# Seven-product blocks for six of the eight column blocks of an MLP's first matrix, in three passes between pieces of the second

## The chip, the cores and the metric

The kernel runs on one core of one Trainium2 chip. The metric is device time in microseconds of one execution. Three runs of the kernel before gave 2460.88 (median), 2460.5 and 2461.72 us.

## The reference

A decoder trunk of two layers on 256 tokens of width 2048, in float32: differential attention, then an MLP; a Mamba-2 mixer, then an MLP. Every sub-layer has an RMS norm ahead of it and a residual behind it. What the change touches is the MLP, which is there twice:

```python
D_MODEL = 2048; SEQ = 256; D_FF = 4 * D_MODEL
def sq_relu_mlp(h, w1, w2):
    return jnp.square(jax.nn.relu(h @ w1)) @ w2
...
h = h + sq_relu_mlp(rms_norm(h, mlp_norm[i]), mlp_w1[i], mlp_w2[i])
```

So per MLP: (256 x 2048) @ (2048 x 8192), a squared ReLU, then (256 x 8192) @ (8192 x 2048).

## The kernel before

**Precision.** Every weight tile is split in two float32r parts: `split_weights` lets ScalarE cast 128 x 1024 elements to the high part (L155) and VectorE subtract it from the raw tile for the low part (L156). Activations are split likewise (`split_pair`, L244 and L245). A product is then three: high x high, activation low x weight high, activation high x weight low.

**The wide form of the first matrix.** `wide_one` and `sub_part` compute one block of 128 hidden columns for all 256 tokens: weights stationary, activations streaming, 16 k-steps. Each k-step is one matmul over 512 columns (high and low activations side by side, L166) and one over 256 (L170). The outcome has hidden units on partitions, as the second matrix needs it. `add_sums` adds the two halves.

**The seven-product form.** For 1024 hidden columns, tokens, inner dimension and columns are each cut in half, and seven products take the place of eight, as in Strassen's scheme in Winograd's variant. `sum_parts` forms the four sums of activations (S1 to S4, split, eight tiles `sa`). `seven` takes 256 rows of the matrix at a time: it loads four 512-column pieces, forms four sums of weights on VectorE (L547 to L550), splits all seven (L540, L541) and issues 7 x 3 matmuls of 512 columns into seven open sums in seven of the eight PSUM banks (L554 to L556). `seven_out` combines them on VectorE (L567 to L573). The outcome has tokens on partitions, so `hidden` applies the squared ReLU (L587) and transposes it on PE, 16 transposes per 1024 columns (L597).

**The order of an MLP.** Four quarters `q` of 2048 hidden columns each. In the first half of a quarter, the eight calls of `seven` for one column block of 1024 alternate with the eight wide blocks of another. Half of the first matrix is so computed by seven products. In the second half, `token_block` multiplies the hidden tiles by the second matrix: for each of four column groups j, eight pieces of 128 x 1024 weights, 12 matmuls of 512 columns each (L227, L229), and VectorE adds the outcome to the residual h (L636).

**Queues.** `side.tick()` runs a step of waiting side work (the sums of activations, `hidden`, the norms) at fixed points of the program. Tiles are named by a tag and a number of buffers: `raw` (loaded weights) and `w` (split weights) have four each, `raw7` two; PSUM has four banks `mm`, three `aux` and one `aux1`. The build lays out each engine's instructions in a fixed order: the program's order is the priority, and an instruction whose inputs or buffer would not be ready yet lets later ones go ahead. All weight loads are issued in order on SP's queue.

Of the kernel before, what the change touches and what calls it, by code (L numbers as in the profile page):

```python
# [12 lines left out]
F32 = mybir.dt.float32  # L13
# [7 lines left out]
P = 128  # L21
# [11 lines left out]
HPG = 8  # L33
SP = 64
MASKED = -1.0e30


C_MIX0, C_MLP0, C_MIX1, C_MLP1 = 0, 16, 32, 48
# [10 lines left out]
def bc(ap, n):  # L49

    return ap.unsqueeze(1).broadcast_to([ap.shape[0], n, ap.shape[1]])
# [31 lines left out]
def wait(n):  # L83
    for _ in range(n):
        yield
# [3 lines left out]
def trunk_kernel(ctx: ExitStack, tc: tile.TileContext, x, xt, par, rope, qk, wv, wo, w10, w10s, w20, win, wdt, wout, w11, w11s, w21, out):  # L89
# [99 lines left out]
    def wide_pair(src, b, acts):  # L189
# [7 lines left out]
                    sub_part(w[t], acts, 8 * s, pp[t], i, s == 0, s == 1)  # L197
        return pp

    def wide_one(src, b, acts):  # L200
        pp = bank()
        raw = [load(src[b, s]) for s in range(2)]
        for s in range(2):
            sub_block(split_weights(raw[s]), acts, 8 * s, pp, s == 0, s == 1)
        return pp
# [4 lines left out]
            S.copy(out=dst[:, t, :], in_=pp[t][:, 1, :])  # L210
            V.tensor_tensor(out=dst[:, t, :], in0=pp[t][:, 0, :], in1=dst[:, t, :], op=ALU.add)

    def token_block(src, j, acts):

        pp = [bank().rearrange("p a b -> p (a b)") for _ in range(2)]
        n = len(src)
        for s in range(n):
            w = split_weights(load(src[s][j]))
            for i, wi in enumerate(w):
                for k in range(2):  # L220
                    while len(acts) <= 2 * s + k:
                        side.tick()
                    act = acts[2 * s + k]
                    m = wi[:, k * NB:(k + 1) * NB]
                    for t in range(2):
                        tok = slice(t * P, (t + 1) * P)
                        PE.matmul(pp[t], lhsT=act[:, 0, tok], rhs=m, start=(s + i + k == 0), stop=(s == n - 1 and i + k == 2))  # L227
                        if i == 0:
                            PE.matmul(pp[t], lhsT=act[:, 1, tok], rhs=m, start=False, stop=False)  # L229
                    if i == 0 or k:  # L230
                        side.tick()
        return pp

    def rng(src, a, b):
# [270 lines left out]

    def sum_parts(pool, x, dst):

        a = pool.tile([P, 2, T], F32, tag="relu", bufs=2, name="a")
        for i in range(2):
            V.tensor_tensor(out=a[:, i, :], in0=x[i][:, 0, :].bitcast(F32), in1=x[i][:, 1, :].bitcast(F32), op=ALU.add)  # L510
        a11, a21, a12, a22 = (a[:, i, t * P:(t + 1) * P] for i in range(2) for t in range(2))
        f = pool.tile([P, 4, P], F32, tag="relu", bufs=2, name="asum")
        yield
        V.tensor_tensor(out=f[:, 0, :], in0=a21, in1=a22, op=ALU.add)
        V.tensor_tensor(out=f[:, 1, :], in0=f[:, 0, :], in1=a11, op=ALU.subtract)
        V.tensor_tensor(out=f[:, 2, :], in0=a11, in1=a21, op=ALU.subtract)
        V.tensor_tensor(out=f[:, 3, :], in0=a12, in1=f[:, 1, :], op=ALU.subtract)
        yield
        sa = pool.tile([P, 2, 4, P], F32R, tag="sa", bufs=8, name="sa")
        S.copy(out=sa[:, 0], in_=f)  # L520
        V.tensor_tensor(out=sa[:, 1], in0=f, in1=sa[:, 0].bitcast(F32), op=ALU.subtract)
        x0, x1 = x
        s1, s2, s3, s4 = ([sa[:, i, n, :] for i in range(2)] for n in range(4))
        dst.append([[x0[:, i, 0:P] for i in range(2)], s4, [x1[:, i, 0:P] for i in range(2)], s1, s3, s2, [x1[:, i, P:T] for i in range(2)]])
        yield

    def seven(pool, src, acts, pp, start, stop):


        r = pool.tile([P, 7, NB], F32, tag="raw7", bufs=2, name="raw7")  # L530
        nc.sync.dma_start(out=r[:, 0:3, :], in_=src[:, 0:3, :])
        nc.sync.dma_start(out=r[:, 6, :], in_=src[:, 3, :])
        ws = []

        def parts(a, n):
            if n == 2:
                w = wp.tile([P, 2, 2, NB], F32R, tag="w", bufs=4, name="w")
            else:
                w = pool.tile([P, 2, 1, NB], F32R, tag="w1", bufs=2, name="w1")
            S.copy(out=w[:, 0], in_=r[:, a:a + n, :])  # L540
            V.tensor_tensor(out=w[:, 1], in0=r[:, a:a + n, :], in1=w[:, 0].bitcast(F32), op=ALU.subtract)  # L541
            for i in range(n):
                ws.append((w[:, 0, i, :], w[:, 1, i, :]))

        parts(0, 2)

        V.tensor_tensor(out=r[:, 3:5, :], in0=r[:, 0:2, :], in1=bc(r[:, 6, :], 2), op=ALU.subtract)  # L547
        parts(2, 2)
        V.tensor_tensor(out=r[:, 5, :], in0=r[:, 1, :], in1=r[:, 3, :], op=ALU.add)
        V.tensor_tensor(out=r[:, 6, :], in0=r[:, 5, :], in1=r[:, 2, :], op=ALU.subtract)  # L550
        parts(4, 2)
        parts(6, 1)
        for n, ((ah, al), (wh, wl)) in enumerate(zip(acts, ws)):
            PE.matmul(pp[n], lhsT=ah, rhs=wh, start=start, stop=False)  # L554
            PE.matmul(pp[n], lhsT=al, rhs=wh, start=False, stop=False)  # L555
            PE.matmul(pp[n], lhsT=ah, rhs=wl, start=False, stop=stop)  # L556
            if n in (1, 3, 5, 6):
                side.tick()

    def seven_out(pool, pp):  # L560

        p1, p3, p2, p5, p7, p6, p4 = pp
        u = pool.tile([P, 2, 2, NB], F32, tag="raw7", bufs=2, name="u")
        a = pool.tile([P, NB], F32, tag="relu", bufs=2, name="ua")
        b = pool.tile([P, NB], F32, tag="relu", bufs=2, name="ub")
        S.copy(out=a, in_=p1)
        V.tensor_tensor(out=u[:, 0, 0], in0=p2, in1=a, op=ALU.add)  # L567
        V.tensor_tensor(out=a, in0=p6, in1=a, op=ALU.add)
        V.tensor_tensor(out=b, in0=p7, in1=a, op=ALU.add)
        V.tensor_tensor(out=u[:, 0, 1], in0=a, in1=p5, op=ALU.subtract)  # L570
        V.tensor_tensor(out=u[:, 0, 1], in0=p3, in1=u[:, 0, 1], op=ALU.add)
        V.tensor_tensor(out=u[:, 1, 1], in0=b, in1=p5, op=ALU.subtract)
        V.tensor_tensor(out=u[:, 1, 0], in0=b, in1=p4, op=ALU.subtract)  # L573
        return u

    def mlp(xs, w1, w1s, w2, pool, after):
        r2 = const.tile([P, 2], F32, tag="r2", bufs=2, name="r2")
# [5 lines left out]
                    yield  # L583
                yield from sum_parts(pool, xs[2 * j:2 * j + 2], sas)

        def hidden(u, hid):
            V.scalar_tensor_tensor(out=u, in0=u, scalar=0.0, in1=u, op0=ALU.max, op1=ALU.mult)  # L587
            yield from wait(2)
            uf = u.rearrange("p t a b -> p t (a b)")
            for j in range(0, 4, 2):  # L590
                axs = []
# [7 lines left out]
                for ax in axs:  # L599
                    hid += split_pair(ax)  # L600
                    yield

        side.add(sums_of(), slow=True)
        for q in range(4):
            hid = []
            p7 = None
            wait_for = 2 if q == 0 else 0
            for j in range(8 + wait_for):
                if j >= wait_for:
                    i = j - wait_for  # L610
                    while len(sas) <= i:
                        side.tick()
                    if i == 0:
                        p7 = [t for _ in range(3) for t in (bank().rearrange("p a b -> p (a b)"), aux())] + [aux1()]
                    seven(pool, w1s[q, i], sas[i], p7, i == 0, i == 7)
                    if i == 7:
                        u = seven_out(pool, p7)
                if j < 8:
                    if j % 2 == 0:
                        r = pool.tile([P, 2, T], F32, tag="relu2", bufs=1, name="relu")  # L620
                    if q or j > 1:
                        add_sums(r[:, j % 2:j % 2 + 1], [wide_one(w1, 8 * q + j, xs)])
                    elif j == 0:
                        add_sums(r, wide_pair(w1, 0, xs))
                    if j % 2:
                        if q == 0 and j == 1:
                            norm_mean()
                            V.reciprocal(out=r2, in_=ms)
                        V.scalar_tensor_tensor(out=r, in0=r, scalar=0.0, in1=r, op0=ALU.max, op1=ALU.mult)
                        hid += split_pair(r)  # L630
            side.add(hidden(u, hid))
            for j in range(4):
                src = rng(w2, 8 * q + 4, 8 * q + 8) + rng(w2, 8 * q, 8 * q + 4)
                pp = token_block(src, j, hid)
                for t in range(2):
                    V.scalar_tensor_tensor(out=h[:, t, cols(j)], in0=pp[t], scalar=r2[:, t:t + 1], in1=h[:, t, cols(j)],  # L636
                                           op0=ALU.mult, op1=ALU.add)
                    if q == 3:
                        after(j, t)

    xs_next = []

# [267 lines left out]
    return _units(b)  # L910


def _mixed(w):

    b = w.reshape(2048, 4, 2, 1024)
    blocks = _blocks(np.ascontiguousarray(b[:, :, 1]).reshape(2048, 4096))
    c = b[:, :, 0].reshape(8, 2, P, 4, 2, 512).transpose(3, 0, 2, 1, 4, 5)
    s = np.stack([c[:, :, :, 0, 0], c[:, :, :, 1, 1], c[:, :, :, 1, 0], c[:, :, :, 0, 1]], axis=3)
    return blocks, np.ascontiguousarray(s)


def _tokens(w):
# [71 lines left out]
```

## Time and profile before

| what | value |
|---|---|
| median of three runs | 2460.88 us |
| the profiled execution's own time | 2460.63 us |
| its span | 2458.7 us |
| busy: PE, VectorE (DVE), ScalarE (ACT) | 100%, 80%, 57% |
| moved by DMA | 471.21 MB, mean 192 GB/s |
| granted TensorE clock | 1.000 |
| first MLP, roughly | 405 to 1100 us |
| second MLP, roughly | 1767 us to the end |

Durations come from the profiled execution. PE's matmuls overlap, so that a matmul's own duration (about 390 ns for 512 columns) is longer than the distance to the next one; the chain of waits gives the distances. PEld are weight loads, which run beside the matmuls. The chain lists, in order of time, the work that ended last; a wait lists who waited for whom.

### The profile page before, as it was taken

To read this page: it belongs to the slowest core of one execution; us is meant where nothing else is said; L and a number is where in the kernel's file an instruction comes from. 1 tells how busy PE (TensorE), PEld (TensorE's weight loads), DVE (VectorE), ACT (ScalarE), POOL (GpSimd) and SP (SyncE) were. 2 spreads that over 40 slices of the span, in tenths; PEclk is the share of its full clock that TensorE was granted. 3 is DMA by queue.
4 is the path that set the end of the run, shared out by engine and by line. 5 is a ranking of instruction groups with operands and counts; after the bars stand their busy time and mean duration, and the time that the engine had idled before them with its cause. 6 is when DMAs were issued, how large, how long until landed. Compare 5 with 4: busy or idle time off the path is not lost.

```text
span 2458.7 us, 33143 instructions
## 1 busy us (share of the span) xinstructions
PE 2452.2 (100%) x12486; PEld 2079.7 (85%) x12486; DVE 1962.1 (80%) x2565; ACT 1406.3 (57%) x2014; POOL 1.2 (0%) x8
## 2 busy tenths in 40 slices
PE   9999999999999999999999999999999999999999
PEld 8888888888888888888888888888888888888887
DVE  6988879977958859758886887887997796795874
ACT  7666656545535536556776575775664454553553
POOL 0000000000000000000000000000000000000000
PEclk9999999999999999999999999999999999999999
DMA  7445555565565655556565555556566556565554
GB/s 271 162 163 180 172 185 181 183 234 194 196 199 189 206 178 199 176 176 208 196 197 192 176 197 197 167 191 210 171 204 217 190 184 214 189 206 197 182 185 156
DMA packets 132128, 471.21 MB, mean 192 GB/s; under 512 B 14752, under 2 KB 14944, under 8 KB 131968
## 3 DMA queue, kind: packets, MB, share of 16 engines
q1 hardware_dynamic: 129248, 460.38, 56.1%
q10 hardware_dynamic: 2720, 8.71, 1.1%
q8 instruction: 98, 1.61, 0.3%
q14 instruction: 62, 0.51, 0.1%
HBM read 466.88 MB, written 2.16 MB: 191 GB/s over the span
## 4 chain that ended last, share of the span: by engine, by line
PE 100%; ACT 0%; DVE 0%; DVEq 0%; issue 0%
PE pp L227 28%; PE pp L166 26%; PE pp L229 14%; PE pp L170 13%; PE aux L554 2%; PE aux L555 2%; PE aux L556 2%; PE pp L555 2%; PE pp L554 2%; PE pp L556 2%; PE aux L796 1%; PE pp L337 1%; PE aux L597 1%; PE aux L428 0%; PE aux L138 0%; PE aux L273 0%
## 5 line engine op out<-in xcount | busy, mean ns | idle before, releaser
L156 DVE TENSOR_TENSOR w<-raw,w 128x1024 fp32r<-128x1024 f32 x730 | 885.4, 1222 | 334.6 <-ACT w L155 332.1
L155 ACT CAST w<-raw 128x1024 fp32r<-128x1024 f32 x730 | 762.4, 1052 | 542.5 <-PE pp L227 433.3
L227 PE MATMUL pp<-w,act 128*128 128x512 f32 x3072 | 957.1, 391 | 0.6 <-ACT w L155 0.6
L166 PE MATMUL pp<-act,w 128*128 128x512 f32 x2768 | 679.3, 392 | 0.0
L227 PEld LDWEIGHTS pp<-w,act 128*128 128x128 f32 x3072 | 575.2, 188 | 120.3 <-issue 1.0
L229 PE MATMUL pp<-w,act 128*128 128x512 f32 x1536 | 598.4, 390 | 0.0
L166 PEld LDWEIGHTS pp<-act,w 128*128 128x128 f32 x2768 | 507.2, 188 | 99.8 <-issue 1.0
L170 PEld LDWEIGHTS pp<-act,w 128*128 128x128 f32 x2768 | 362.6, 191 | 17.9 <-issue 0.9
L170 PE MATMUL pp<-act,w 128*128 128x256 f32 x2768 | 373.2, 283 | 0.0
L540 ACT CAST w<-raw 128x1024 fp32r<-128x1024 f32 (+1 forms) x256 | 241.1, 945 | 200.4 <-PE pp L170 105.7
L229 PEld LDWEIGHTS pp<-w,act 128*128 128x128 f32 x1536 | 288.5, 188 | 58.2
L541 DVE TENSOR_TENSOR w<-raw,w 128x1024 fp32r<-128x1024 f32 (+1 forms) x256 | 272.3, 1087 | 41.5 <-ACT w L540 38.5
L547 DVE TENSOR_TENSOR raw<-raw 128x1024 f32<-128x1024 f32 x64 | 78.1, 1221 | 3.5 <-DMA raw<-in_w11s 1.5
L554 PE MATMUL aux<-w,sa 128*128 128x512 f32 x192 | 75.0, 391 | 0.0
L555 PE MATMUL aux<-w,sa 128*128 128x512 f32 x192 | 74.9, 390 | 0.0
L556 PE MATMUL aux<-w,sa 128*128 128x512 f32 x192 | 74.7, 389 | 0.0
L721 DVE SCALAR_TENSOR_TENSOR cy<-u,cwb,cy 128x256 f32<-128x256 f32 x144 | 63.6, 482 | 9.9 <-ACT cy L719 9.6
L210 ACT COPY relu<-pp 128x256 f32<-128x256 f32 x64 | 23.8, 372 | 59.4 <-PE pp L170 59.3
L636 DVE SCALAR_TENSOR_TENSOR h<-pp,r,h 128x512 f32<-128x512 f32 x64 | 45.1, 747 | 13.0 <-PE pp L227 13.0
L555 PE MATMUL pp<-w,act 128*128 128x512 f32 x128 | 50.3, 393 | 0.0
L554 PE MATMUL pp<-w,act 128*128 128x512 f32 x128 | 50.2, 392 | 0.0
L556 PE MATMUL pp<-w,act 128*128 128x512 f32 x128 | 49.9, 390 | 0.0
(230 smaller groups left out, 1899.8 us busy)
## 6 DMA issues: line engine op xcount, KB each, us to landing
raw<-in_w SPq DMA_DIRECT2D x384, 512.0 KB, 3.7
raw<-in_win SPq DMA_DIRECT2D x160, 512.0 KB, 4.0
raw<-in_wout SPq DMA_DIRECT2D x64, 512.0 KB, 3.4
raw<-in_qk SPq DMA_DIRECT2D x56, 512.0 KB, 3.9
raw<-in_w10s SPq DMA_DIRECT2D x32, 768.0 KB, 4.4
raw<-in_w11s SPq DMA_DIRECT2D x32, 768.0 KB, 4.4
raw<-in_wv SPq DMA_DIRECT2D x32, 512.0 KB, 4.5
raw<-in_wo SPq DMA_DIRECT2D x32, 512.0 KB, 3.9
```

Of the source, the lines that this page charges most:

```text
L155: S.copy(out=wh[:, s], in_=raw[:, s])
L156: V.tensor_tensor(out=wl[:, s], in0=raw[:, s], in1=wh[:, s].bitcast(F32), op=ALU.subtract)
L166: PE.matmul(acc, lhsT=wk, rhs=acts[k0 + k], start=(start and k == 0), stop=False)
L170: PE.matmul(acc[:, 0, :], lhsT=wk, rhs=acts[k0 + k][:, 0, :], start=False, stop=(stop and k == 7))
L227: PE.matmul(pp[t], lhsT=act[:, 0, tok], rhs=m, start=(s + i + k == 0), stop=(s == n - 1 and i + k == 2))
L229: PE.matmul(pp[t], lhsT=act[:, 1, tok], rhs=m, start=False, stop=False)
L540: S.copy(out=w[:, 0], in_=r[:, a:a + n, :])
L541: V.tensor_tensor(out=w[:, 1], in0=r[:, a:a + n, :], in1=w[:, 0].bitcast(F32), op=ALU.subtract)
L547: V.tensor_tensor(out=r[:, 3:5, :], in0=r[:, 0:2, :], in1=bc(r[:, 6, :], 2), op=ALU.subtract)
L554: PE.matmul(pp[n], lhsT=ah, rhs=wh, start=start, stop=False)
L555: PE.matmul(pp[n], lhsT=al, rhs=wh, start=False, stop=False)
L556: PE.matmul(pp[n], lhsT=ah, rhs=wl, start=False, stop=stop)
```

## The change

`MLP_KINDS = "sSSSsSSS"` gives the eight column blocks of 1024 a kind: `s` is computed in the wide form, `S` by seven products. Six of eight are now S, where four were; the second matrix and the splits stay as they are.

An S block is no longer computed in one sweep with seven open sums. It goes in three passes over the inner dimension, each in four steps of 512 rows: first p1 and p5, then p7, p3 and p6, then p2 and p4. So at most three sums are open, in the `aux` and `aux1` banks. Since the passes need the same pieces again, pieces are loaded more than once. Two of the four sums of weights (`wsum` and `t3`) are now formed by loading one piece and letting a DMA on POOL's queue (`G.dma_start` with `accum_op`) add the other; the other two stay on VectorE (`a[i]` is reused). Two signs are turned so that accumulating DMAs only add. Between the passes VectorE combines the finished sums; the squared ReLU goes to ScalarE as two instructions.

`both` yields after each product step (12 matmuls) or half of a wide block. Ahead of the first quarter, blocks 0 and 1 are computed, one s and one S in turn. From then on, the two blocks of the next quarter are computed between the pieces of the second matrix for the present one (`token_steps` yields after each piece; 30 pieces share the steps evenly, after three steps ahead). The last quarter has no such work between its pieces. `expand` makes the hidden tiles of a quarter (the transposes of an S block, the split of both kinds) as side work at the quarter's begin.

```diff
+MLP_KINDS = "sSSSsSSS"
...
+    def wide_steps(src, b, acts, dst):
+        pp = bank()
+        for s in range(2):
+            sub_block(split_weights(load(src[b, s])), acts, 8 * s, pp, s == 0, s == 1)
+            yield
+        add_sums(dst, [pp])
...
-    def token_block(src, j, acts):
+    def token_steps(src, j, acts):
...
                     if i == 0 or k:
                         side.tick()
+            yield pp
...
-        V.tensor_tensor(out=f[:, 0, :], in0=a21, in1=a22, op=ALU.add)
+        V.tensor_tensor(out=f[:, 0, :], in0=a21, in1=a22, op=ALU.subtract)
...
-        V.tensor_tensor(out=f[:, 3, :], in0=a12, in1=f[:, 1, :], op=ALU.subtract)
+        V.tensor_tensor(out=f[:, 3, :], in0=a12, in1=f[:, 1, :], op=ALU.add)
...
-    def seven(pool, src, acts, pp, start, stop):
-    def seven_out(pool, pp):
...
+    def seven(pool, src, sas, u):
+        a = [None] * 4
+        def product(pp, which, w, i):
+            for j, wj in enumerate(w):
+                for kp in range(2):
+                    ah, al = sas[2 * i + kp][which]
+                    m = wj[:, kp * NB:(kp + 1) * NB]
+                    PE.matmul(pp, lhsT=ah, rhs=m, start=(i + kp + j == 0), stop=(i == 3 and kp + j == 2))
+                    if j == 0:
+                        PE.matmul(pp, lhsT=al, rhs=m, start=False, stop=False)
+        A11, S4, A12, S1, S3, S2, A22 = range(7)
+        p1, p5 = aux(), aux()
+        for i in range(4):
+            while len(sas) < 2 * i + 2:
                 side.tick()
+            a[i] = pool.tile([P, 1024], F32, tag="wsum", bufs=4, name="wsum")
+            nc.sync.dma_start(out=a[i], in_=src[1, i])
+            G.dma_start(out=a[i], in_=src[0, i], accum_op=ALU.add)
+            w = split_weights(load(src[0, i]))
+            product(p1, A11, w, i)
+            yield
+            product(p5, S1, split_weights(a[i]), i)
+            yield
+        S.copy(out=u[:, 0, 0], in_=p1)
+        S.copy(out=u[:, 1, 1], in_=p5)
+        p7, p3, p6 = aux(), aux1(), aux()
+        for i in range(4):
+            t3 = pool.tile([P, 1024], F32, tag="acc", bufs=2, name="t3")
+            nc.sync.dma_start(out=t3, in_=src[1, i])
+            G.dma_start(out=t3, in_=src[2, i], accum_op=ALU.add)
+            b22 = load(src[2, i])
+            product(p7, S3, split_weights(t3), i)
+            yield
+            product(p3, S4, split_weights(b22), i)
+            yield
+            V.tensor_tensor(out=a[i], in0=b22, in1=a[i], op=ALU.add)
+            product(p6, S2, split_weights(a[i]), i)
+            yield
...
+        p2, p4 = aux(), aux()
+        for i in range(4):
+            b21 = load(src[3, i])
+            product(p2, A12, split_weights(b21), i)
+            yield
+            V.tensor_tensor(out=a[i], in0=a[i], in1=b21, op=ALU.add)
+            product(p4, A22, split_weights(a[i]), i)
+            yield
...
+        uf = u.rearrange("p t a b -> p (t a b)")
+        S.activation(uf, uf, AF.Relu)
+        S.activation(uf, uf, AF.Square)
+        yield
...
+        def both(q, share):
+            if not share:
+                yield from hidden(2 * q)
+                yield from hidden(2 * q + 1)
+                return
+            a, b = hidden(2 * q), hidden(2 * q + 1)
+            for _ in range(4):
+                next(a)
+                yield
+            due = 0.0
+            for _ in a:
+                due += share
+                yield
+                while due >= 1:
+                    due -= 1
+                    next(b, None)
+                    yield
+            yield from b
...
+        for _ in both(0, 28 / 12 if kinds[:2] == "sS" else 1.0):
+            pass
...
         for q in range(4):
             hid = []
...
+            for c in (2 * q, 2 * q + 1):
+                side.add(expand(c, hid))
+            work = iter(())
+            rate = 0.0
+            if q < 3:
+                n = sum(16 if k == "s" else 29 for k in kinds[2 * q + 2:2 * q + 4])
+                work, rate = both(q + 1, 0), n / 30
+                for _ in range(3):
+                    next(work)
+                    side.tick()
+            due = 0.0
             for j in range(4):
...
+                for pp in token_steps(src, j, hid):
+                    due += rate
+                    while due >= 1:
+                        due -= 1
+                        next(work, None)
...
-    w10, w10s = _mixed(a["mlp_w1"][0])
+    w10, w10s = _mixed(a["mlp_w1"][0], MLP_KINDS)
```

More of the change, by code (lines that the diff above doesn't have):

```diff
@@ L231, in token_block @@
                         side.tick()
+            yield pp
+    def token_block(src, j, acts):
+        for pp in token_steps(src, j, acts):
+            pass
         return pp
@@ L506, in sum_parts @@
     def sum_parts(pool, x, dst):
-        a = pool.tile([P, 2, T], F32, tag="relu", bufs=2, name="a")
+        a = pool.tile([P, 1024], F32, tag="acc", bufs=2, name="a")[:, 0:512].rearrange("p (a b) -> p a b", a=2)
         for i in range(2):
@@ L511, in sum_parts @@
         a11, a21, a12, a22 = (a[:, i, t * P:(t + 1) * P] for i in range(2) for t in range(2))
-        f = pool.tile([P, 4, P], F32, tag="relu", bufs=2, name="asum")
+        f = pool.tile([P, 1024], F32, tag="acc", bufs=2, name="asum")[:, 0:512].rearrange("p (a b) -> p a b", a=4)
         yield
-        V.tensor_tensor(out=f[:, 0, :], in0=a21, in1=a22, op=ALU.add)
+        V.tensor_tensor(out=f[:, 0, :], in0=a21, in1=a22, op=ALU.subtract)
         V.tensor_tensor(out=f[:, 1, :], in0=f[:, 0, :], in1=a11, op=ALU.subtract)
         V.tensor_tensor(out=f[:, 2, :], in0=a11, in1=a21, op=ALU.subtract)
-        V.tensor_tensor(out=f[:, 3, :], in0=a12, in1=f[:, 1, :], op=ALU.subtract)
+        V.tensor_tensor(out=f[:, 3, :], in0=a12, in1=f[:, 1, :], op=ALU.add)
         yield
@@ L525, in sum_parts @@
         yield
-    def seven(pool, src, acts, pp, start, stop):
[L530 to L557, printed above, removed]
-                side.tick()
@@ L560, in seven_out @@
-    def seven_out(pool, pp):
[L562 to L570, printed above, removed]
-        V.tensor_tensor(out=u[:, 0, 1], in0=p3, in1=u[:, 0, 1], op=ALU.add)
-        V.tensor_tensor(out=u[:, 1, 1], in0=b, in1=p5, op=ALU.subtract)
-        V.tensor_tensor(out=u[:, 1, 0], in0=b, in1=p4, op=ALU.subtract)
-        return u
+    def seven(pool, src, sas, u):
[12 more added lines that the diff above has]
+            while len(sas) < 2 * i + 2:
+                side.tick()
+            a[i] = pool.tile([P, 1024], F32, tag="wsum", bufs=4, name="wsum")
[21 more added lines that the diff above has]
+            yield
+        V.tensor_tensor(out=u[:, 0, 1], in0=p6, in1=u[:, 0, 0], op=ALU.add)
+        V.tensor_tensor(out=u[:, 1, 0], in0=p7, in1=u[:, 0, 1], op=ALU.add)
+        V.tensor_tensor(out=u[:, 0, 1], in0=u[:, 1, 1], in1=u[:, 0, 1], op=ALU.subtract)
+        V.tensor_tensor(out=u[:, 0, 1], in0=p3, in1=u[:, 0, 1], op=ALU.add)
+        V.tensor_tensor(out=u[:, 1, 1], in0=u[:, 1, 1], in1=u[:, 1, 0], op=ALU.subtract)
+        p2, p4 = aux(), aux()
[6 more added lines that the diff above has]
+            yield
+        V.tensor_tensor(out=u[:, 0, 0], in0=p2, in1=u[:, 0, 0], op=ALU.add)
+        V.tensor_tensor(out=u[:, 1, 0], in0=p4, in1=u[:, 1, 0], op=ALU.add)
+        uf = u.rearrange("p t a b -> p (t a b)")
+        S.activation(uf, uf, AF.Relu)
+        S.activation(uf, uf, AF.Square)
+        yield
@@ L584, in sums_of, with blocks, hidden, expand @@
                 yield from sum_parts(pool, xs[2 * j:2 * j + 2], sas)
-        def hidden(u, hid):
-            V.scalar_tensor_tensor(out=u, in0=u, scalar=0.0, in1=u, op0=ALU.max, op1=ALU.mult)
-            yield from wait(2)
+        def blocks(c, u):
+            r = u.rearrange("p t a b -> p (t a b)").rearrange("p (j a b) -> p j a b", j=4, a=2)
+            for j in range(8):
+                yield from wide_steps(w1, 8 * c + j, xs, r[:, j // 2, j % 2:j % 2 + 1])
+                if j % 2:
+                    S.activation(r[:, j // 2], r[:, j // 2], AF.Relu)
+                    S.activation(r[:, j // 2], r[:, j // 2], AF.Square)
+        kinds = MLP_KINDS
+        us = {}
+        def hidden(c):
+            us[c] = u = pool.tile([P, 2, 2, NB], F32, tag="u", bufs=2, name="u")
+            n = kinds[:c].count(kinds[c])
+            if kinds[c] == "s":
+                yield from blocks(n, u)
+            else:
+                yield from seven(pool, w1s[n], sas, u)
+        def expand(c, hid):
+            u = us.pop(c)
+            if kinds[c] == "s":
+                r = u.rearrange("p t a b -> p (t a b)").rearrange("p (j a b) -> p j a b", j=4, a=2)
+                for j in range(4):
+                    hid += split_pair(r[:, j])
+                    yield
+                return
             uf = u.rearrange("p t a b -> p t (a b)")
@@ L601, in hidden @@
                     yield
+        def both(q, share):
+            if not share:
+                yield from hidden(2 * q)
+                yield from hidden(2 * q + 1)
+                return
+            a, b = hidden(2 * q), hidden(2 * q + 1)
[9 more added lines that the diff above has]
+                    next(b, None)
+                    yield
+            yield from b
@@ L603, in mlp @@
         side.add(sums_of(), slow=True)
+        for _ in both(0, 28 / 12 if kinds[:2] == "sS" else 1.0):
+            pass
+        norm_mean()
+        V.reciprocal(out=r2, in_=ms)
         for q in range(4):
             hid = []
[L606 to L630, printed above, removed]
@@ L635, in mlp @@
+            due = 0.0
+            for j in range(4):
+                src = rng(w2, 8 * q, 8 * q + 8)
+                for pp in token_steps(src, j, hid):
[3 more added lines that the diff above has]
+                        next(work, None)
                 for t in range(2):
@@ L639, in mlp @@
                         after(j, t)
+            for _ in work:
+                pass
     xs_next = []
@@ L910, in _blocks, with _mixed @@
     return _units(b)
[L913 to L919, printed above, removed]
+def _mixed(w, kinds):
+    b = w.reshape(2048, 8, 1024)
+    blocks = _blocks(np.ascontiguousarray(b[:, [i for i in range(8) if kinds[i] == "s"]]).reshape(2048, -1))
+    c = b[:, [i for i in range(8) if kinds[i] == "S"]]
+    c = c.reshape(4, 2, 2, P, -1, 2, 512).transpose(4, 0, 3, 1, 2, 5, 6)
+    s = np.stack([c[:, :, :, :, 0, 0], c[:, :, :, :, 0, 1], c[:, :, :, :, 1, 1], c[:, :, :, :, 1, 0]], axis=1)
+    return blocks, np.ascontiguousarray(s).reshape(-1, 4, 4, P, 1024)
 def _tokens(w):
@@ L974 @@
     rope = np.ascontiguousarray(np.stack([np.concatenate([cos, cos]), np.concatenate([-sin, sin])], axis=1).astype(f32))
-    w10, w10s = _mixed(a["mlp_w1"][0])
-    w11, w11s = _mixed(a["mlp_w1"][1])
+    w10, w10s = _mixed(a["mlp_w1"][0], MLP_KINDS)
+    w11, w11s = _mixed(a["mlp_w1"][1], MLP_KINDS)
     args = {
```

3 lines of the change are left out of this document (removed).

## The prediction

> **What bounds the kernel now.** I read the page's busy line and chain first, then the view of the waits, then the chain's pieces, then the groups by form, then windows and transfers.
>
> ```profile
> span 2458.7 us, 33143 instructions
> PE 2452.2 (100%) x12486; PEld 2079.7 (85%) x12486; DVE 1962.1 (80%) x2565; ACT 1406.3 (57%) x2014; POOL 1.2 (0%) x8
> PE 100%; ACT 0%; DVE 0%; DVEq 0%; issue 0%
> ```
>
> The chain that ended last is PE from end to end. The view of PE's waits has four rows in all:
>
> ```profile
> PE warm L113 <- DVE ones_r L106: 1.1, 1, 1.1
> PE pp L227 <- ACT w L155: 0.6, 1, 0.6
> PE aux L138 <- DVE sqr L133: 0.2, 1, 0.2
> PE aux L138 <- ACT sqr L132: 0.2, 1, 0.2
> ```
>
> That is 2.1 us of waiting. So time is the sum of what PE issues, as long as it stays fed, and the question has two halves: how much PE work goes, and whether the feeding still keeps up. Busy times overlap on PE, so I price by the pieces of the chain (start, length, what):
>
> ```profile
> 1106.87 3.65 PE pp L166 x16
> 1110.53 1.91 PE pp L170 x16
> 497.06 1.31 PE aux L597 x12
> 502.04 1.13 PE pp L227 x5
> 504.76 1.13 PE pp L227 x5
> 507.48 1.13 PE pp L227 x5
> ```
>
> A k-step of a wide block is one L166 (3.65/16 = 228 ns) and one L170 (1.91/16 = 119 ns): 347.5 ns. L227's runs of five start 2.72 us apart, and that is one piece of the second matrix, 12 matmuls of 512 columns: 226.7 ns each. A transpose is 1.31/12 = 109 ns. (The pair of rows at 1106 lies in the state-space layer, with the same instruction and shape.)
>
> **The change part by part.** *PE, the sum.* Per MLP, six column blocks of 1024 instead of four go by seven products, so four blocks change over in the two MLPs. A wide block is 8 x 16 k-steps: 128 x 347.5 ns = 44.5 us. By products it is 7 x 8 x 3 = 168 matmuls of 512 columns: 168 x 226.7 ns = 38.1 us, and its outcome is token-major, so 16 transposes come with it: 1.75 us. Saved per block 44.5 - 38.1 - 1.75 = 4.65 us; four blocks, 18.6 us. The eight blocks that were products before keep their 168 matmuls and 16 transposes; only their order changes (three passes instead of seven open sums). The second matrix keeps its matmuls. Nothing else is removed from PE, so 18.6 us is the most that this can bring, and it hangs on the cover.
>
> *VectorE and ScalarE.* Prices:
>
> ```profile
> L156 DVE TENSOR_TENSOR w<-raw,w 128x1024 fp32r<-128x1024 f32 x730 | 885.4, 1222 | 334.6 <-ACT w L155 332.1
> L155 ACT CAST w<-raw 128x1024 fp32r<-128x1024 f32 x730 | 762.4, 1052 | 542.5 <-PE pp L227 433.3 <-PE pp L170 52.4 <-issue 17.2
> L547 DVE TENSOR_TENSOR raw<-raw 128x1024 f32<-128x1024 f32 x64 | 78.1, 1221 | 3.5 <-DMA raw<-in_w11s 1.5 <-DMA raw<-in_w10s 1.5
> L550 DVE TENSOR_TENSOR raw<-raw 128x512 f32<-128x512 f32 x64 | 44.2, 690 | 1.6
> L567 DVE TENSOR_TENSOR u<-pp,ua 128x512 f32<-128x512 f32 x8 | 5.5, 686 | 0.8 <-PE pp L556 0.7
> L636 DVE SCALAR_TENSOR_TENSOR h<-pp,r,h 128x512 f32<-128x512 f32 x64 | 45.1, 747 | 13.0 <-PE pp L227 13.0
> L245 DVE TENSOR_TENSOR act<-aux,act 128x512 fp32r<-128x512 f32 x32 | 20.6, 687 | 0.4 <-ACT act L244 0.4
> L587 DVE SCALAR_TENSOR_TENSOR u<-u 128x2048 f32<-128x2048 f32 x8 | 18.3, 2287 | 0.0
> ```
>
> A block by products after: 28 splits x 1.222 = 34.2, 8 sums left on VectorE x 1.221 = 9.8, 7 combinations x 0.686 = 4.8: 48.8 us of VectorE for 38.1 us of PE. Before, the sums were 8 x (1.221 + 2 x 0.690) = 20.8, and the squared ReLU 2.3 more, which now goes to ScalarE as two instructions; by L155's 1.03 ns per element I estimate 2 x 2.1 us there. VectorE is thus slower than PE on such a block, and the new order hides this by laying two blocks between the 32 pieces of the second matrix. A quarter with two product blocks: PE 32 x 2.72 + 2 x 38.1 + 1.75 = 165 us; VectorE 32 x 1.222 + 8 x 0.747 + 8 x 0.687 + 2 x 48.8 = 148 us, 0.90. (With all four sums on VectorE, 16 more at 1.221, it would be 168, over PE: the two sums by DMA earn nothing themselves, they keep the cover.) ScalarE: 32 + 2 x 28 = 88 casts x 1.052 = 93 us, plus some 15 for ReLUs and copies, 0.65. Is 0.90 enough? The windows of before (length, then busy of PE, PEld, DVE, ACT, POOL; clock; DMA share; GB/s):
>
> ```profile
> 415.00:510.00 95.00, 95.00 (x470) 79.70 (x469) 91.90 (x118) 55.79 (x70) 0.00 (x0) 1.00 0.57 201
> 490.00:505.00 15.00, 15.00 (x76) 12.58 (x75) 15.00 (x17) 7.21 (x9) 0.00 (x0) 1.00 0.76 266
> 505.00:520.00 15.00, 15.00 (x67) 12.40 (x67) 12.48 (x15) 6.44 (x7) 0.00 (x0) 1.00 0.81 286
> 11.00:16.00 5.00, 5.00 (x32) 4.45 (x31) 3.44 (x8) 3.17 (x7) 0.00 (x0) 1.00 1.05 395
> ```
>
> At the start of an MLP VectorE was busy 91.9 of 95 us, with PE busy all 95. So 0.90 costs nothing by that row. At the start itself the new order asks 34.2 + 20.8 + 4.8 + 2.3 - 48.8 = 13.3 us less of VectorE than the old one. I take 0.
>
> *Transfers.* A product block loads 28 pieces of 512 KB where it loaded 16 (two matrices are read again for the accumulation, one more for its own product): 12 blocks x 12 x 0.524 = 75 MB more than the 471 now. Eight of the 28 accumulate, issued on POOL's empty queue; the other 20 go through SP, four more than the 16 issues of before. Prices:
>
> ```profile
> q1 hardware_dynamic: 129248, 460.38, 56.1%
> raw<-in_w SPq DMA_DIRECT2D x384, 512.0 KB, 3.7
> ab<-dram_a ACTq DMA_DIRECT2D x16, 512.0 KB, 6.4
> SPq L183 <- DVE w L156: 1437.6, 644, 12.4
> ```
>
> The fastest rate is that of the window 11 to 16: 395 GB/s, with the share full; I take 390, so 0.524/0.390 = 1.34 us of all engines for a piece. Quarter with two product blocks: 32 + 2 x 20 = 72 plain pieces, 97 us, and 16 accumulations. No accumulation is in the trace. Its floor is a plain piece, 1.34 us; the ceiling is the slowest of the steady 512 KB rows, the broadcast with 6.4 us, taken as if nothing ran beside it. I take two plain pieces, 2.7 us, since it reads two tiles and writes one, by bytes near the floor: 97 + 16 x 2.7 = 140 of 165 us, 0.85, against the 0.81 in 505 to 520 where PE lost nothing. The first block pair (16 + 20 plain, 8 accumulating) needs 48 + 22 = 70 of 82.6 us. Cost 0. The break-even is (165 - 97)/16 = 4.2 us.
>
> [...]
>
> *Latency.* An accumulation waits on POOL for its load (3.7 us), and its split waits for it. Only accumulations queue behind it there. The four wsum tiles come free in the third pass of the block before, eight product steps ahead of their use: 8 x 2.72 us plus some four pieces between, 33 us, against 3.7 + 2.7 and an issue. The two acc tiles have six steps plus three pieces, 24 us. SP's queue is in order and waits for free buffers already (1437.6 us in all, without PE seeing it). A wsum load that waits for its buffer now holds the loads of the second matrix behind it; four split tiles of 2.72 us each cover 11 us. I take 0 here.
>
> *New waits on PE.* The three aux banks are shared: while two hold products, a transposed pair gets one bank until a pass ends. This meets the quarters with two product blocks, twice per MLP; four split tiles are ready work, so I take 0.5 us each, 2 us (between 0 and one evacuation and split, 2 x 0.69 + 0.6). The last quarter of each MLP begins with transposes, a cast and a subtraction (L245, 0.687) before its first matmul, with no product step to cover it; before, half of the hidden pairs were ready by then. I take 1.2 us each, 2.4 us. Sum: -18.6 + 2 + 2.4 = -14.2 us on the profiled execution's 2460.63, whose median is 2460.88: 2446.5 us.
>
> **The rivals.** *Slower: transfers become the bound.* If an accumulation holds the engines longer than 4.2 us, PE waits in the product quarters. At 5.4 us (four plain pieces), 97 + 86 = 183: 18 us in each of two quarters, and 48 + 43 = 91 against 82.6 at the start: 45 us per MLP, 90 in all, 2535 us. At the ceiling of 6.4 it would be 2616. For it: nothing in the trace accumulates, and 0.81 is already reached. Against: by bytes it needs 2.7.
>
> *Slower: accumulations come late.* If each is held until VectorE pauses, as long as the 15 us without a pause in 490 to 505, 16 of them in a row on POOL are 240 us for a quarter of 165: 75 us in each of four quarters, about 2740. Against: a single delay of 15 us fits in the 24 us of lead.
>
> [...]
>
> *Slower by a little: the order misses.* The engines' orders are fixed at build; if loads or sums come later than planned, each of 12 product blocks may lose 2 us or more at its pass ends: 24 - 14 = 10 us slower, 2470 us.
>
> *No change.* The same at some 1 us per block: 12 us, 2458 us. For it: three evacuations per block instead of one. Against: PE's waits of 2.1 us with seven sums open at once.
>
> **How the numbers follow.** A difference under 0.2%, 4.9 us, is about what a measurement cannot tell from none. Forecast 0.62 (from the full 18.6 us, 2442, to 2456); no change 0.13; transfers the bound 0.13; late accumulations 0.04; order misses 0.08. So faster 0.62, same 0.13, slower 0.25. The range leaves out the two dear cases' far ends, about 0.15, and some 0.03 below: 2440 to 2485. The forecast's own range is 2441 to 2456.
>
> **What would show it.** Right: L166 falls from 2768 to 2256 instructions, products rise from 1344 to 2016 matmuls, transposes of the hidden tiles from 128 to 192, bytes by 75 MB (more, if the accumulating reads are counted), PE's waits stay under some 10 us, and the DMA share in a product quarter is below 0.9. Wrong: waits of PE on ACT or DVE whose own wait is an accumulation on wsum or t3; a share near 1.0 in those quarters; VectorE at 1.0 there while PE pauses. A gain above 20 us would mean that PE's price per matmul fell, which nothing here foretells.

## The result, and the profile after

The changed kernel takes 2540.0 us (median; 2532.8 to 2551.8) against 2460.9 us: a ratio of 1.033, interval 1.0302 to 1.035. It is 79 us slower where 14 us less was forecast, and outside the range. Its profiled execution took 2539.03 us, with a span of 2537.3 us.

The page after, its busy line, its transfer queues and its chain:

```profile
span 2537.3 us, 32938 instructions
PE 2470.3 (97%) x12198; PEld 2062.2 (81%) x12198; DVE 1937.0 (76%) x2441; ACT 1504.3 (59%) x2070; POOL 83.2 (3%) x104
...
q1 hardware_dynamic: 136160, 485.55, 56.5%
q0 software_dynamic: 13824, 50.34, 11.1%
...
PE 62%; DMA 18%; DVE 13%; issue 4%; ACT 2%; DVEq 0%; SPq 0%; ACTq 0%
```

PE was the whole chain before; now DMA, VectorE and ScalarE hold a third of it. VectorE is less busy than before over the whole (76% against 80%), so it is not the first suspect. PE stands idle for 2537.3 - 2470.3 = 67 us, where it was 6.5. The view of waits names who PE waited for, and behind those, who the feeders waited for (total, times, longest):

```profile
ACT w L158 <- DMA raw<-in_w: 55.6, 36, 5.3
...
DVE wsum L583 <- DMA raw<-in_w11s: 42.9, 20, 4.5
...
PE aux L554 <- DVE w L159: 31.8, 21, 5.2
...
PE aux L652 <- DVE act L261: 12.0, 6, 3.8
PE aux L652 <- ACT u L603: 9.0, 2, 4.8
```

ScalarE's wait for `raw<-in_w` was this before:

```profile
ACT w L155 <- DMA raw<-in_w: 9.0, 3, 4.6
```

So ordinary loads (`in_w` is the second matrix and the wide blocks of the first), which the change does not touch, land late: 36 times instead of 3. Two pieces of the chain show how lateness gets to PE. The first lies in the second quarter, where blocks 4 and 5 are computed ahead, among the steps of block 5 (start, length, what):

```profile
801.47 5.84 DMA raw<-in_w10s
...
808.48 1.23 DVE w L159
809.71 0.02 issue
809.73 6.65 DMA raw<-in_w10s
816.38 0.02 issue
816.40 0.04 ACTq L158
816.43 0.04 issue
816.48 1.05 ACT w L158
817.53 0.01 issue
817.54 2.35 DVE w L159 x2
```

VectorE frees a raw buffer, the next load starts at once, takes 6.65 us, and ScalarE and VectorE then need over 2 us more. The ring of four buffers goes round on the landing time; PE has run dry by then, from 815.5 to 818.8 us. The second piece is at the end of the first pair of blocks:

```profile
490.93 9.28 DMA wsum<-in_w10s
...
500.29 0.07 ACT w L158
500.36 0.88 issue
501.24 1.91 ACT u L603
503.15 0.04 issue
503.20 0.65 PE aux L652 x4
503.85 0.39 PE pp L238
504.24 0.43 PE aux L554
504.67 0.43 PE aux L556
...
507.50 0.23 PE pp L238
```

An accumulation of 9.28 us holds a cast on ScalarE; the squared ReLU of the finished block is queued behind that cast; the transposes wait for it. And after the pause matmuls come 0.43 us apart instead of 0.23, for some 3.5 us. The windows (length, busy of PE, PEld, DVE, ACT, POOL; granted clock; DMA share; GB/s) show a lower clock after another pause, in the last row. The first row, most of the quarter that computes blocks 2 and 3, shows that the DMA engines were not full on average; the second shows that they were in stretches:

```profile
500.00:665.00 165.00, 158.26 (x682) 126.41 (x683) 130.35 (x123) 94.79 (x95) 13.57 (x16) 0.99 0.89 265
...
660.00:680.00 20.00, 16.61 (x83) 14.02 (x82) 13.39 (x15) 12.94 (x14) 1.70 (x2) 0.95 1.03 314
...
920.00:940.00 20.00, 16.79 (x66) 13.71 (x67) 18.81 (x19) 8.23 (x9) 1.70 (x2) 0.83 0.76 230
```

The trace has nine stretches at half clock in this execution, 44 us together, where the kernel before has a mean clock of 1.000; by that I estimate some 22 us of PE time.

### The profile page after: what moved, and what is told of

Same layout as the page of the kernel before. It is cut to its first block, busy times and chain, and to the rows that moved or that the text cites. A ratio compares the mean times of both kernels' runs of the same rounds, so it can differ in the third digit from the quotient of the medians.

```text
span 2537.3 us, 32938 instructions
## 1 busy us (share of the span) xinstructions
PE 2470.3 (97%) x12198; PEld 2062.2 (81%) x12198; DVE 1937.0 (76%) x2441; ACT 1504.3 (59%) x2070; POOL 83.2 (3%) x104
## 3 DMA queue, kind: packets, MB, share of 16 engines
q0 software_dynamic: 13824, 50.34, 11.1%
## 4 chain that ended last, share of the span: by engine, by line
PE 62%; DMA 18%; DVE 13%; issue 4%; ACT 2%; DVEq 0%; SPq 0%; ACTq 0%
PE pp L169 19%; PE pp L238 17%; DVE w L159 10%; PE pp L173 10%; PE pp L240 9%; DMA raw<-in_w10s 7%; DMA raw<-in_w11s 7%; DMA raw<-in_w 4%; ACT w L158 2%; PE aux L554 2%; PE aux L556 1%; DVE wsum L596 1%; PE aux L652 1%; PE aux L866 1%; DVE h L704 1%
## 5 line engine op out<-in xcount | busy, mean ns | idle before, releaser
L159 DVE TENSOR_TENSOR w<-raw,w 128x1024 fp32r<-128x1024 f32 x810 | 980.9, 1220 | 301.2 <-ACT w L158 296.2
L238 PE MATMUL pp<-w,act 128*128 128x512 f32 x3072 | 989.0, 393 | 4.2 <-ACT w L158 3.0
L240 PE MATMUL pp<-w,act 128*128 128x512 f32 x1536 | 601.0, 391 | 1.3 <-DVE act L261 1.3
L169 PE MATMUL pp<-act,w 128*128 128x512 f32 x2256 | 556.5, 394 | 0.0
L169 PEld LDWEIGHTS pp<-act,w 128*128 128x128 f32 x2256 | 414.8, 189 | 82.2 <-issue 1.0
L173 PEld LDWEIGHTS pp<-act,w 128*128 128x128 f32 x2256 | 293.0, 191 | 14.8 <-DVE w L159 1.7
L554 PE MATMUL aux<-w,sa 128*128 128x512 f32 x768 | 260.5, 395 | 8.8 <-DVE w L159 8.2
L158 ACT CAST w<-wsum 128x1024 fp32r<-128x1024 f32 x144 | 151.3, 1051 | 128.0 <-DVE wsum L596 46.9
L554 PE MATMUL aux<-w,act 128*128 128x512 f32 x576 | 202.4, 404 | 24.5 <-DVE w L159 23.6
L159 DVE TENSOR_TENSOR w<-wsum,w 128x1024 fp32r<-128x1024 f32 x144 | 175.6, 1219 | 26.5 <-ACT w L158 25.3
L554 PEld LDWEIGHTS aux<-w,sa 128*128 128x128 f32 x768 | 144.0, 189 | 44.7 <-DVE w L159 14.6
L554 PEld LDWEIGHTS aux<-w,act 128*128 128x128 f32 x576 | 108.2, 192 | 58.3 <-DVE w L159 35.4
L556 PE MATMUL aux<-w,sa 128*128 128x512 f32 x384 | 150.8, 393 | 0.0
L556 PE MATMUL aux<-w,act 128*128 128x512 f32 x288 | 113.7, 395 | 0.0
L596 DVE TENSOR_TENSOR wsum<-wsum,raw 128x1024 f32<-128x1024 f32 x48 | 57.8, 1221 | 55.6 <-DMA raw<-in_w10s 29.1
L556 PEld LDWEIGHTS aux<-w,sa 128*128 128x128 f32 x384 | 72.7, 189 | 15.0
```

What stands on the lines that cost most here:

```text
L158: S.copy(out=wh[:, s], in_=raw[:, s])
L159: V.tensor_tensor(out=wl[:, s], in0=raw[:, s], in1=wh[:, s].bitcast(F32), op=ALU.subtract)
L169: PE.matmul(acc, lhsT=wk, rhs=acts[k0 + k], start=(start and k == 0), stop=False)
L173: PE.matmul(acc[:, 0, :], lhsT=wk, rhs=acts[k0 + k][:, 0, :], start=False, stop=(stop and k == 7))
L554: PE.matmul(pp, lhsT=ah, rhs=m, start=(i + kp + j == 0), stop=(i == 3 and kp + j == 2))
L556: PE.matmul(pp, lhsT=al, rhs=m, start=False, stop=False)
```

## The experiments

**Theory A**: the accumulating DMAs hold the DMA engines, ordinary loads land late, four raw buffers do not reach far enough ahead, and PE pauses. **Theory B**: the new order itself starves PE (three passes, shared banks, ReLU on ScalarE, pieces loaded twice).

### No accumulations

```diff
-            G.dma_start(out=a[i], in_=src[0, i], accum_op=ALU.add)
...
-            G.dma_start(out=t3, in_=src[2, i], accum_op=ALU.add)
```

> The changed kernel without its 96 accumulating DMAs: the wsum and t3 tiles hold one piece only, so two of the four weight sums are left out. PE's work and all plain loads stay. Theory A (the accumulations hold the DMA engines, the plain loads land late, PE pauses): the pauses go, 2443 to 2460 us, PE's waits under 10 us. Theory B (the new order itself starves PE: three passes, shared banks, ReLU on ScalarE, pieces loaded twice): 2500 to 2540 us, PE's waits near the 60 us of the changed kernel.

Measured: 2450.5 us, ratio 0.9957 (0.9942 to 0.9972). The costliest row of PE's waits is this:

```profile
PE pp L240 <- DVE act L261: 1.3, 2, 0.7
```

Theory B falls: the order, the passes and the second loading of pieces keep PE fed. All 89.5 us hang on the 96 accumulations.

### The sums on VectorE

```diff
-            G.dma_start(out=a[i], in_=src[0, i], accum_op=ALU.add)
-            w = split_weights(load(src[0, i]))
+            b11 = load(src[0, i])
+            w = split_weights(b11)
...
+            V.tensor_tensor(out=a[i], in0=b11, in1=a[i], op=ALU.add)   # ahead of p5's product
...
-            G.dma_start(out=t3, in_=src[2, i], accum_op=ALU.add)
             b22 = load(src[2, i])
+            V.tensor_tensor(out=t3, in0=t3, in1=b22, op=ALU.add)       # behind b22's load
```

> All four weight sums on VectorE, the two new ones from the raw tiles that are loaded anyway; no accumulating DMA, the reference's result. VectorE then has 168 us of work in a quarter of 165 with two product blocks. Theory A: 2450 to 2475 us, some 3 us lost to VectorE in each of four quarters. Theory B, or VectorE as the new bound with its queue behind: 2490 to 2530 us.

Measured: 2451.3 us, ratio 0.996 (0.9945 to 0.9975): 0.4% faster than the kernel before, a small gain but clear of the scatter, and 0.8 us from the one without the sums. Its page and the window of the quarter:

```profile
PE 2438.6 (100%) x12198; PEld 2055.8 (84%) x12198; DVE 2038.8 (83%) x2537; ACT 1506.7 (62%) x2070; POOL 1.2 (0%) x8
...
500.00:665.00 165.00, 165.00 (x755) 137.08 (x755) 153.97 (x149) 102.86 (x105) 0.00 (x0) 1.00 0.71 237
```

VectorE is busy 154 of 165 us and PE all of them. The prediction had counted 168 for it and concluded that two sums had to go elsewhere. They had not. It is not that work was left out of this window: it holds 149 VectorE instructions where the count has 150, and their durations add up to 164 us. But durations overlap on VectorE too. Back to back, two instructions of 1.22 us start 1.13 us apart:

```profile
568.85 1.22 DVE L159 TENSOR_TENSOR w<-wsum,w 128x1024 fp32r<-128x1024 f32 x1
569.98 1.22 DVE L569 TENSOR_TENSOR wsum<-raw,wsum 128x1024 f32<-128x1024 f32 x1
```

### What of an accumulation costs: double time, bytes, or the chain

An accumulation adds three things: bytes, the time of the add, and a chain (load, then POOL, then the split). Four kernels separate them. *Copying on POOL* drops `accum_op` in both lines. *Aside* lets POOL load or accumulate the same bytes into a tile that nobody reads:

```diff
-            G.dma_start(out=a[i], in_=src[0, i], accum_op=ALU.add)
+            for c in range(2):
+                G.dma_start(out=scratch, in_=src[0, i][:, 512 * c:512 * c + 512])   # or with accum_op=ALU.add
```

and *small* accumulates 128 of the 1024 columns in place. The t3 line is changed likewise.

> The same 96 DMAs on POOL's queue, with the same bytes and waits, but copying in place of adding (the two sums are left out). Theory A1 (it is the double engine time of an accumulation, 328 ns per 4 KB packet against 159): most of the loss goes, 2450 to 2475 us, and the queue's packets take about 160 ns. Theory A2 (it is the extra bytes and the chain load, POOL, load): it stays at 2510 to 2540 us. Theory B: 2500 to 2540 us.

> As without accumulations (two sums left out), and POOL loads the same bytes at the same places of the program into a scratch tile that nobody reads, in halves of 256 KB, by copying. Nobody waits for them; only the bytes are there. Theory T (the engines' time: other loads land later): near the kernel that copied on POOL, 2475 to 2500 us. Theory C (the chain of load, POOL, load makes the sums late): as without accumulations, 2449 to 2458 us.

> The same, but the loads into the scratch tile accumulate, so the engines' double time is there and the chain is not (two sums left out). Theory T: 2510 to 2545 us, near the changed kernel's 2540. Theory C: 2449 to 2460 us.

> The accumulating DMAs at their places and with their waits, but only 128 of the 1024 columns (64 KB): most of the two sums is left out. The chain is there, an eighth of the bytes is. Theory T: 2450 to 2463 us. Theory C: 2480 to 2530 us.

| kernel | bytes | add | chain | us | above 2450.5 |
|---|---|---|---|---|---|
| small, in place | an eighth | an eighth | yes | 2457.2 | 7 |
| copying, aside | yes | no | no | 2469.6 | 19 |
| copying on POOL | yes | no | yes | 2492.1 | 42 |
| accumulating, aside | yes | yes | no | 2504.9 | 54 |
| the changed kernel | yes | yes | yes | 2540.0 | 90 |

The page's queue of POOL's DMAs, copying (first) and accumulating aside (second); the third number is the share of 16 engines' span:

```profile
q0 software_dynamic: 13824, 50.34, 5.8%
```

```profile
q0 software_dynamic: 27648, 50.34, 12.3%
```

With the changed kernel's 11.1% above, that is 0.111 x 2537 / 96 = 2.93 us of all engines per accumulation against 0.058 x 2493 / 96 = 1.51 us per copy: an add costs twice a copy. Two pairs in the table differ by the add alone: it costs 48 us on POOL with the chain (2492.1 to 2540.0) and 35 us aside. The aside kernels are not quite the same bytes at the same time, though. Their halves all go to one tile, and each waits for the one before:

```profile
POOL scratch L566 <- DMA scratch<-in_w10s: 258.3, 47, 7.3
```

So they are spread over the MLP, the stretch of the wide block included, where the changed kernel has no accumulation (680 to 760 us). With that said, bytes and adds that nobody waits for make 54 us. The chain alone makes 7. Together in place they make 90, which is more than 54 + 7: the rest comes of both at once, and how much of it is the chain and how much the closer spacing was not separated. Nor was a copy of the same bytes on SP's queue tried, so that what belongs to the bytes and what to POOL's queue stays open. Most expectations that named one cause alone missed: copying on POOL was put at 2475 at most or 2510 at least, copying aside at 2458 at most or 2475 at least, and both fell between; accumulating aside was put at 2460 at most or 2510 at least, and fell between too. Only the small accumulation came as the engines' time alone would have it.

### Half of the accumulations

```diff
-            G.dma_start(out=t3, in_=src[2, i], accum_op=ALU.add)
             b22 = load(src[2, i])
+            V.tensor_tensor(out=t3, in0=t3, in1=b22, op=ALU.add)
```

> Only the t3 sum on VectorE, the wsum sum still by accumulating DMA (48 in place of 96). Theory A: about half of the loss, 2465 to 2505 us. Theory B: 2510 to 2545 us. If VectorE is what PE waits for, it is slower than with both sums by DMA.

Its mirror puts the wsum sum on VectorE instead, as in the kernel above, and leaves t3 to the DMAs.

> The mirror of the kernel with only the t3 sum on VectorE (2479.7 us): now wsum on VectorE and t3 by 48 accumulating DMAs, the reference's result. Theory T (the engines' time counts, whichever tile): 2470 to 2490 us. If it is the depth of the buffers that decides (t3 has two, wsum four, and the sum of t3 has 6 product steps of lead, that of wsum 8): later than its mirror, 2490 to 2520 us.

Measured: 2479.7 us with wsum alone accumulated, 2507.8 us with t3 alone. Above 2451.3 that is 28 and 56 us, together 85 of the 89. Engine time is nearly the same in both (48 accumulations, 5.5% and 5.8% of the span), so the lead counts too: t3 has two buffers and six product steps, wsum four and eight. When only t3 accumulates, PE's waits show the first one of each MLP, which a cast waits for directly (second row):

```profile
PE aux L554 <- DVE w L159: 17.9, 18, 3.5
PE aux L554 <- ACT w L158: 10.8, 2, 5.9
```

### One raw buffer more

```diff
-        raw = wp.tile([P, 1024], F32, tag="raw", bufs=4, name="raw")
+        raw = wp.tile([P, 1024], F32, tag="raw", bufs=5, name="raw")
```

For the space, the tile `dg` shares its buffer with `junk`, and `tri` is made in the state-space layer.

> The changed kernel with five raw buffers in place of four (the space comes from two small constant tiles); all accumulations stay, the reference's result. If PE pauses because four buffers look too short a way ahead once loads land late: one more piece, 2.7 us of cover against pauses of 1 to 5 us, takes half of the loss or more, 2480 to 2515 us. If the engines' share over a whole quarter is the bound, depth does not help: 2530 to 2545 us.

> All sums on VectorE, no accumulation, and five raw buffers, the reference's result. With loads that land in time, depth is worth little: 2447 to 2452 us beside the 2451.3 us with four.

Measured: 2504.5 us with the accumulations, 36 us less than with four buffers. With the same bytes and engine time, one piece more of lead takes 40% of the 90 us, and ScalarE's waits for ordinary loads fall from 55.6 us to this:

```profile
ACT w L156 <- DMA raw<-in_w: 16.5, 17, 2.5
```

So engine time over a whole quarter is not the bound; what counts is whether each load lands in time. Without accumulations the fifth buffer brings nothing: 2455.5 us, 4 us more than with four, a miss. That kernel also has the moved small tiles; which of these costs the 4 us was not separated.

### Seven blocks, and GpSimd as the adder

Both kernels start from the one with all sums on VectorE.

```diff
-MLP_KINDS = "sSSSsSSS"
+MLP_KINDS = "sSSSSSSS"
```

> All sums on VectorE, and seven of the eight column blocks by products (two more in the two MLPs): 9.3 us of PE less, and one more quarter per MLP in which VectorE has 168 us for 165. If VectorE at its limit costs the 1 us that separates the kernel with sums on VectorE from the one without the sums: 2442 to 2447 us. If the third such quarter makes VectorE the bound: 2450 us or more.

Measured: 2464.0 us, ratio 1.0009 (1.0 to 1.0018): the first case missed, and the time falls in the second. In the windows of two neighbouring quarters with two product blocks, PE no longer fills its time:

```profile
500.00:665.00 165.00, 162.52 (x717) 132.16 (x716) 154.06 (x146) 101.42 (x101) 0.00 (x0) 1.00 0.68 228
665.00:835.00 170.00, 167.38 (x736) 136.48 (x737) 152.32 (x146) 101.40 (x100) 0.00 (x0) 0.99 0.67 220
```

That VectorE is the bound there is not shown: 154 of 165 us is what it had above, where PE was full. The costliest row of PE's waits is the split of the hidden tiles on VectorE, at the start of the second and the third quarter of each MLP:

```profile
PE aux L554 <- DVE act L261: 10.1, 4, 2.8
```

A quarter with a wide block, where VectorE has less to do, may be what this kernel lacks; no run tests it. To relieve VectorE otherwise:

```diff
-            V.tensor_tensor(out=t3, in0=t3, in1=b22, op=ALU.add)
+            G.tensor_tensor(out=t3, in0=t3, in1=b22, op=ALU.add)
```

> No accumulating DMA; wsum on VectorE, the t3 sum as an addition of GpSimd (48 instructions of 128x1024), the reference's result. If POOL's additions run beside VectorE's: VectorE falls to 158 of 165 us in a quarter with two product blocks, 2447 to 2452 us. [...]

Measured: 2533.9 us, 83 us more than with that sum on VectorE. The group of the additions, then VectorE's subtraction L159 (min/median/max) with GpSimd adding, and last in the changed kernel, where GpSimd only issues DMAs:

```profile
L579 POOL TENSOR_TENSOR t<-t,raw 128x1024 f32<-128x1024 f32 x48 | 158.8, 3311 | 2202.2 <-DVE ms L312 847.7
...
L159 DVE TENSOR_TENSOR w<-raw,w x810: 1193/1218/3434, 33.4 to 2517.1; 128x1024 fp32r<-128x1024 f32 x162
```

```profile
L159 DVE TENSOR_TENSOR w<-raw,w x810: 1193/1219/1228, 32.8 to 2523.0; 128x1024 fp32r<-128x1024 f32 x162
```

An addition takes 3.3 us, and a subtraction of VectorE takes up to 3.4 us in this run, where the longest is 1.24 with all sums on VectorE and 1.23 in the changed kernel. So the case of 2447 to 2452 us missed: with GpSimd adding, single subtractions of VectorE took nearly three times as long. How that comes about is not shown. The 96 DMAs that GpSimd issues in the changed kernel left VectorE's durations alone (1219 ns in the median, 1228 at most). How much of the 83 us is VectorE's delay and how much the later sum (3.3 us where VectorE takes 1.22) was not separated.

## Why the prediction was wrong, point by point

- **PE's work: the counts right, the gain half there.** L169 ran 2256 times, the products 768 + 576 + 384 + 288 = 2016 times, the hidden tiles' transposes 192 times, and bytes rose by 546.7 - 471.2 = 75.5 MB. With the sums on VectorE, 9.6 us of the 18.6 arrive. PE's idle time rises by 4.6 us there (11.1 against 6.5), about the 4.4 that were put for small waits; its busy time falls by only 13.6, and where the other 5 went was not traced.
- **VectorE's cover: right in that 0.90 costs nothing, wrong in what it concluded.** Four sums there were counted at 168 us for 165 and took 154 of a window of 165, because the count adds up durations that overlap. The accumulations were not needed to keep the cover.
- **Transfers, cost 0: this step failed.** The price was nearly right (2.7 us put, 2.93 measured; 140 of 165 us or 0.85 put, a share of 0.89 measured) and stayed below the break-even of 4.2 us. The break-even itself was the error: it asks whether the engines have time enough over a quarter, and not whether each load lands in time. What was put at 0 here and in the next point cost 90 us together. A share of 0.71 kept PE fed and one of 0.89, with 20 us at 1.03 at the quarter's end, did not, with four buffers; with five, 36 us of the loss went. That PE had lost nothing in 15 us at 0.81 before said little about a whole quarter.
- **Latency, cost 0: the second step that failed.** The two legs of a wsum were put at 3.7 and 2.7 us; the view of the DMAs after says 7.0 and 8.6. A t3 has 5.2 and 7.5:

```profile
wsum<-in_w10s SPq DMA_DIRECT2D x24, 512.0 KB, 7.0
wsum<-in_w10s POOLq DMA_DIRECT2D x24, 512.0 KB, 8.6
t<-in_w10s SPq DMA_DIRECT2D x24, 512.0 KB, 5.2
t<-in_w10s POOLq DMA_DIRECT2D x24, 512.0 KB, 7.5
```

  Landing times of a less loaded kernel were used for a more loaded one. The lead was shorter than put as well: from the issue of a tile's first load to its first cast the trace has a median of 26 us for wsum (33 put) and 17 for t3 (24 put). So most of the sums still came in time, and t3 was the one that casts waited for:

```profile
ACT w L158 <- DMA t<-in_w11s: 17.9, 6, 4.4
...
ACT w L158 <- DMA t<-in_w10s: 14.9, 6, 4.4
```

  ScalarE's waits for ordinary loads come to more than that, 55.6 us against 32.8. What is queued behind a waiting cast on ScalarE (the squared ReLU, and with it the transposes) was not named at all.
- **The rivals.** "Transfers become the bound" gave 2535 us at 5.4 us per accumulation; the time fits by chance, since the price was 2.93. Nor is the loss where that rival had it: it put 26 us by the end of the first quarter, 18 in the third, and named none for the second, which has one product block. Against the kernel without accumulations, the last addition to the residual in these quarters of the first MLP comes 22, 34 and 42 us later: 22, 11 and 9 us more in each. "Accumulations come late" had the right place and the wrong reason: a hold until VectorE pauses was the author's supposition, and no run shows one. An issue takes 0.86 us, and the trace has each accumulation issued within 1.2 us of its load's landing:

```profile
L565 POOL DMA_DIRECT2D wsum<-in_w10s x24 | 20.6, 858 | 527.8 <-DMA wsum<-in_w10s 460.4 <-DVE w L159 51.1 <-DVE u L590 13.5
```

- **The add's double time.** An accumulation took 2.93 us of all engines, a copy 1.51. The forecast's two plain pieces, 2.7 us, were the author's estimate from what a sum reads and writes; no run shows those reads, only the time. So it had nearly this price, and left out what it does to the loads beside it.

## What to carry to other kernels

A mean DMA share below one was no cover here (0.89 in a quarter with two product blocks). Count, for each ring of buffers, landing time plus the steps that free a buffer against the time that its pieces keep PE busy, and take landing times from a stage that is as loaded as the planned one. Before work is taken from a busy engine to one that others share, make the kernel that leaves it there: here VectorE at 83% could do all sums, and of the kernels with the full outcome that one was the fastest. And count an engine's work by the distance from one instruction to the next where rows show it, not by durations (on VectorE here 1.13 us against 1.22).

## What the runs showed of the hardware that was not expected

PE's pauses cost more than their length. In the changed kernel, with pauses of 2.6 to 5.2 us, the granted clock fell to one half for 3.4 or 6.8 us, nine times; matmuls of 512 columns came 0.43 us apart there, and 0.23 apart otherwise. That is some 22 of the 90 us by the estimate above. Copying on POOL, where the longest wait named is 2.9 us, has a mean clock of 0.998, where the kernel before has 1.000. The shortest of the nine pauses, 2.6 us (PE resumes at 1960.3 us), was enough; what decides which pause is followed by half clock was not separated. The window with the pause's end:

```profile
1960.00:1980.00 20.00, 19.73 (x79) 15.89 (x80) 19.13 (x20) 9.17 (x9) 2.22 (x3) 0.91 0.90 268
```
